# The second level of the RWKV join made for all four blocks of 32, with one evacuation each, and the norm's bias added with the bonus

## The chip, the cores and the metric

The kernel runs on one core of a Trainium2 chip. A core has a matrix engine, TensorE (PE in the profile; its weight loads are listed apart as PEld), three engines for elementwise work, VectorE (DVE), ScalarE (ACT) and GpSimd (POOL), and SyncE (SP), which issues most of the DMAs. Each engine takes its own instructions in the order of the program and stops where one of them has to wait. The metric is the device time of one execution in microseconds; the median of three runs of the kernel before is 3190.79 us (3189.75 to 3197.08).

## The reference

The reference is a model of two parts: two layers of a first network (528 tokens, width 1024), and one layer of a second network. Every layer of the first projects the tokens, runs attention (MLA) and a bidirectional RWKV mixer beside each other, joins them and runs a mixture of experts. The change lies in the RWKV mixer alone. Cut to that:

```python
def step(S, inp):
    r_t, w_t, k_t, v_t, kk_t, b_t = inp
    sa = jnp.einsum('bhvk,bhk->bhv', S, kk_t)
    S = S * w_t[:, :, None, :] - sa[..., None] * b_t[:, :, None, :] + v_t[..., None] * k_t[:, :, None, :]
    return S, jnp.einsum('bhvk,bhk->bhv', S, r_t)
...
bonus = jnp.sum(rh * kd * r_k, -1, keepdims=True) * vh
...
y = y_f + y_b
mu = jnp.mean(y, -1, keepdims=True)
var = jnp.mean(jnp.square(y - mu), -1, keepdims=True)
yn = ((y - mu) * lax.rsqrt(var + RWKV_GN_EPS)).reshape(B, L, RW) * gn_g + gn_b
out = (yn + (bonus_f + bonus_b).reshape(B, L, RW)) * g
```

There are eight heads of 64, and the scan runs once forward and once backward.

## The kernel before

The scan is done in nine chunks of 64 tokens. Inside a chunk the recurrence is a triangular system with a matrix of 64x64 per head; the kernel computes the inverse T of that matrix, and with it the chunk becomes a few products. A unit is one pair of heads p (0 to 3) in one direction d, so a layer has eight units, 0 to 7, unit i being p = i // 2, d = i % 2. Both layers run the same program, so there are 16 units.

The work of a unit passes through these generators:

- `rwkv_front` (L744) makes the decays and keys. It uses ACT, POOL and DVE. Its scan is L779, its longest steps are L798 on DVE and L800 on POOL, which write the tile rbk; in the backward direction POOL adds the two directions' keys (L813) and DVE makes the bonus's product (L815). L751 scales the keys on ACT for a new pair of heads, and L776 is POOL's first step of it.
- `rwkv_gen` (L820) makes the products KR (L834, DVE) and the chunk matrices Z (L846 on PE, L849 on DVE). After the backward direction `rwkv_bonus` (L867) replaces v by the bonus.
- `rwkv_inv` (L911) inverts the diagonal blocks of 16x16 on DVE (L924, L926), with DMAs before and after it.
- `rwkv_join` (L940) makes T from them in two levels. The first joins blocks of 16 to blocks of 32 (tile TB: four blocks of 32 on the 128 partitions, two heads by two halves, times eight chunks). Its products are Q (L959) and U (L967); L962 and L968 evacuate them on DVE. The second level joins blocks of 32 to 64: Q2 (L979) and U2 (L987) are made for one of the two halves of each head, so for two of the four partition quarters. ACT evacuates the quarter of the first head (L981, L988), DVE that of the second (L982, L989). The diagonal of T comes from TB by two ACT instructions (L970), each with a mask for one half.
- `rwkv_kx` (L992) and `rwkv_solve` (L1007) apply T: PE's products L1016 read the tile rtt, which is T.
- `rwkv_scan` (L1033) runs over the chunks: PE's L1069 and L1072, with DVE's L1070 between two chunks.
- `rwkv_post` (L1086) runs once for a pair of heads: mean, variance, the norm's scale (L1106, DVE), its bias (L1112, POOL), the bonus (L1114, POOL), and the gate's product (PE) that DVE multiplies in (L1118). It does so half by half of the 528 tokens. For p = 3, which runs after the last unit, one DVE instruction (L1109) does bias and bonus.

In `rwkv` (L1122) PE and DVE are set to the order in which the code is written. `spread` interleaves the generators' steps, up to each `yield`, by the weights given with them. In unit i the streams are the chain (solve and scan of unit i), the work behind it (gen of i+2, kx of i+2, front of i+3), inv and join of unit i+1, and in units 2, 4 and 6 the post step of the pair before. Join 0 comes ahead of unit 0. ACT, POOL and SP, and everything outside this part, get their order from a scheduler when the program is built.

Of the kernel before, what the change touches and what calls it, by code (L numbers as in the profile page):

```python
# [115 lines left out]
class K:  # L116
# [749 lines left out]

    def rwkv_bonus(self, S, G):  # L867
        nc = self.nc
        bs, v = G["bs"], S["v"][G["p"]]
        for c0, n in HALVES:  # L870
            ps = self.pa("bo", "r")
            nc.tensor.matmul(ps[:, :n], lhsT=self.blk1, rhs=bs[:, c0:c0 + n], start=True, stop=True)
            vv = v[:, PAD + c0:PAD + c0 + n]
            nc.vector.tensor_tensor(out=vv, in0=ps[:, :n], in1=vv, op=ALU.mult)
        yield

# [63 lines left out]
    def rwkv_join(self, S, G):  # L940
# [8 lines left out]
        def q4(g):  # L949
            return slice(32 * g, 32 * g + 32)  # L950
# [17 lines left out]
        nc.vector.tensor_tensor(out=TB, in0=TB, in1=ps[:, :8], op=ALU.add)  # L968
        for e in range(2):
            nc.scalar.activation(out=T[:, 1:9, 32 * e:32 * e + 32], in_=TB, func=AF.Copy, scale=self.par32[:, e:e + 1])  # L970
        yield
# [4 lines left out]
        for c in range(8):  # L976
            for h in range(2):
                g = 2 * h
                nc.tensor.matmul(ps[q4(g + 1), c], lhsT=Zx[h][q4(g), c + 1, 32:64], rhs=D[q4(g), c], start=True, stop=True)  # L979
        Q = self.t("rq", (128, 8, 32))  # L980
        nc.scalar.copy(Q[q4(1)], ps[q4(1), :8])  # L981
        nc.vector.tensor_copy(Q[q4(3)], ps[q4(3), :8])  # L982
        yield
        ps = self.pa("U2", "r").rearrange("p (c t) -> p c t", t=32)
        for c in range(8):
            for g in (0, 2):
                nc.tensor.matmul(ps[q4(g), c], lhsT=Q[q4(g + 1), c], rhs=TB[q4(g + 1), c], start=True, stop=True)  # L987
        nc.scalar.copy(T[q4(0), 1:9, 32:64], ps[q4(0), :8])  # L988
        nc.vector.tensor_copy(T[q4(2), 1:9, 32:64], ps[q4(2), :8])  # L989
        yield  # L990
# [95 lines left out]
    def rwkv_post(self, li, p, S, role):  # L1086
# [15 lines left out]
        for c0, n in HALVES:  # L1102
            q = slice(c0, c0 + n)
            ps = self.pa("hb", role)
            nc.tensor.matmul(ps[:, :n], lhsT=self.sel[:2, 0], rhs=rn[:2, q], start=True, stop=True)
            nc.vector.scalar_tensor_tensor(out=y[:, q], in0=y[:, q], scalar=self.col(f"gng{li}", p), in1=ps[:, :n], op0=ALU.mult,  # L1106
                                           op1=ALU.mult)
            if p == 3:
                nc.vector.scalar_tensor_tensor(out=y[:, q], in0=y[:, q], scalar=self.col(f"gnb{li}", p), in1=v[:, q], op0=ALU.add,  # L1109
                                               op1=ALU.add)  # L1110
            else:
                nc.gpsimd.tensor_scalar(out=y[:, q], in0=y[:, q], scalar1=self.col(f"gnb{li}", p), scalar2=0.0, op0=ALU.add,  # L1112
                                        op1=ALU.add)
                nc.gpsimd.tensor_tensor(out=y[:, q], in0=y[:, q], in1=v[:, q], op=ALU.add)  # L1114
            ps = self.pa("g", role)
            nc.tensor.matmul(ps[:, :n], lhsT=S["g2"][:, p * 128:(p + 1) * 128], rhs=S["gd"][:, PAD + c0:PAD + c0 + n], start=True,
                             stop=True)
            nc.vector.tensor_tensor(out=out[:, q], in0=y[:, q], in1=ps[:, :n], op=ALU.mult)  # L1118
            yield
        S["out"].append(out)  # L1120

    def rwkv(self, li, u, rn, nb, freed):  # L1122
# [17 lines left out]
        def gen(i):  # L1140
            if i <= last:
                yield from self.rwkv_gen(li, S, G[i])
                if units[i][1]:
                    yield from self.rwkv_bonus(S, G[i])

# [1727 lines left out]
```

## Time and profile before

| what | value |
|---|---|
| median of three runs | 3190.79 us |
| the profiled execution's own time | 3186.1 us |
| its span | 3184.2 us |
| PE, busy (share of the span) | 2716.5 us (85%) |
| DVE, busy | 1559.3 us (49%) |
| POOL, busy | 1231.7 us (39%) |
| ACT, busy | 1085.6 us (34%) |
| RWKV stage of layer 0 | about 320 to 663 us |
| RWKV stage of layer 1 | about 1395 to 1728 us |

How to read it: the shares are means over stages with different limits. In a view of the order of time each line is one instruction or several of one kind merged (x64 at its end): start and length in us, engine, line of the kernel, operation, the tile written and the tiles read, the shape, and in brackets how long the engine had been idle before it and which instruction ended that wait. A wait for several things is put down to the one that came last. For PE every product of fp32 operands shows as two records. In the view of stretches a line gives the length, then the busy time of PE, PEld, DVE, ACT and POOL with their counts, the granted PE clock as a share of full speed, the busy share of the DMA engines and the rate.

### The profile page before, as it was taken

To read this page: it belongs to the slowest core of one execution; us is meant where nothing else is said; L and a number is where in the kernel's file an instruction comes from. 1 tells how busy PE (TensorE), PEld (TensorE's weight loads), DVE (VectorE), ACT (ScalarE), POOL (GpSimd) and SP (SyncE) were. 2 spreads that over 40 slices of the span, in tenths; PEclk is the share of its full clock that TensorE was granted. 3 is DMA by queue.
4 is the path that set the end of the run, shared out by engine and by line. 5 is a ranking of instruction groups with operands and counts; after the bars stand their busy time and mean duration, and the time that the engine had idled before them with its cause. 6 is when DMAs were issued, how large, how long until landed. Compare 5 with 4: busy or idle time off the path is not lost. (4 is left out here: it accounts for less than half of the span.)

```text
span 3184.2 us, 54720 instructions
## 1 busy us (share of the span) xinstructions
PE 2716.5 (85%) x21572; PEld 2070.2 (65%) x21572; DVE 1559.3 (49%) x3328; ACT 1085.6 (34%) x2377; POOL 1231.7 (39%) x1276
## 2 busy tenths in 40 slices
PE   6998777888799499977778797779888999999998
PEld 5887655664354388856656533267676788778886
DVE  6575665543123427666653511144866667344412
ACT  4233433211232322244322111143335665244431
POOL 3124233052344322332323311047865544555554
PEclk8997776787899699978778799989999999999999
DMA  6220100348899615211114599932121124423343
GB/s 188 60 90 19 24 13 12 107 147 319 339 364 382 224 47 160 78 32 19 16 56 157 195 415 420 372 135 84 61 72 34 61 70 146 146 86 97 96 123 103
DMA packets 224043, 443.17 MB, mean 139 GB/s; under 512 B 96576, under 2 KB 105152, under 8 KB 197136
## 3 DMA queue, kind: packets, MB, share of 16 engines
q1 hardware_dynamic: 209648, 407.76, 36.8%
q0 software_dynamic: 9216, 25.44, 2.1%
q10 hardware_dynamic: 4912, 6.34, 0.5%
q8 instruction: 175, 2.87, 0.4%
q14 instruction: 92, 0.75, 0.1%
HBM read 400.91 MB, written 46.61 MB: 141 GB/s over the span
## 5 line engine op out<-in xcount | busy, mean ns | idle before, releaser
L230 POOL TENSOR_TENSOR wl<-wr,wh 128x512 fp32r<-128x512 f32 x328 | 435.5, 1329 | 535.3 <-ACT wh L229 505.1
L229 ACT CAST wh<-wr 128x512 fp32r<-128x512 f32 x352 | 217.5, 619 | 551.2 <-PE mm L336 208.2
L335 PE MATMUL mm<-hh,wh 128*128 128x264 f32 x608 | 186.1, 306 | 19.2 <-ACT hf L290 13.0
L335 PE MATMUL mm<-h,wh 128*128 128x512 f32 x480 | 187.6, 391 | 2.2 <-ACT h L229 2.2
L337 PE MATMUL mm<-h,wl 128*128 128x512 f32 x480 | 187.7, 391 | 1.2 <-POOL wl L230 1.2
L336 PE MATMUL mm<-h,wh 128*128 128x512 f32 x480 | 187.4, 390 | 0.3 <-DVE h L230 0.3
L337 PE MATMUL mm<-hh,wl 128*128 128x264 f32 x608 | 181.0, 298 | 0.0
L336 PE MATMUL mm<-hl,wh 128*128 128x264 f32 x608 | 179.5, 295 | 0.0
L1461 POOL DMA_INDIRECT ybuf<-my,rdst x32 | 32.3, 1009 | 278.5 <-DVE my L1460 247.6
L335 PEld LDWEIGHTS mm<-hh,wh 128*128 128x128 f32 x608 | 118.6, 195 | 29.6 <-ACT hf L290 13.6
L335 PE MATMUL go<-h,wh 128*128 128x512 f32 x288 | 121.1, 420 | 13.1 <-ACT th L2145 8.7
L1432 DVE SCALAR_TENSOR_TENSOR mth<-mth,w 128x256 f32<-128x256 f32 x32 | 13.5, 421 | 236.7 <-ACT mth L1431 236.7
L224 POOL TENSOR_SCALAR rs<-s 128x4 f32<-128x4 f32 (+7 forms) x62 | 14.7, 238 | 273.4 <-DVE s L723 196.0
L336 PEld LDWEIGHTS mm<-hl,wh 128*128 128x128 f32 x608 | 118.5, 195 | 2.6 <-issue 1.3
L337 PEld LDWEIGHTS mm<-hh,wl 128*128 128x128 f32 x608 | 118.3, 195 | 2.3 <-issue 1.3
L1443 PE MATMUL w<-mw,xT 128*64 128x512 f32 x344 | 113.7, 615 | 6.5 <-DMA mw<-in_moe_w_dram 6.3
L337 PE MATMUL go<-h,wl 128*128 128x512 f32 x288 | 116.1, 403 | 0.0
L336 PE MATMUL go<-h,wh 128*128 128x512 f32 x288 | 115.0, 399 | 0.0
L335 PEld LDWEIGHTS mm<-h,wh 128*128 128x128 f32 x480 | 90.5, 189 | 21.2 <-ACT h L229 2.5
L337 PEld LDWEIGHTS mm<-h,wl 128*128 128x128 f32 x480 | 90.4, 188 | 20.8 <-POOL wl L230 2.0
L336 PEld LDWEIGHTS mm<-h,wh 128*128 128x128 f32 x480 | 90.5, 189 | 19.4 <-issue 0.6
L1652 DVE SCALAR_TENSOR_TENSOR ma<-hf,sc,ma 128x512 f32<-128x512 f32 x112 | 94.5, 862 | 17.5 <-DMA hf<-in_w_mod_dram 16.8
(610 smaller groups left out, 7454.1 us busy)
## 6 DMA issues: line engine op xcount, KB each, us to landing
mw<-in_moe_w_dram SPq DMA_DIRECT2D x61, 1024.0 KB
mz<-in_moe_w_dram SPq DMA_DIRECT2D x48, 1024.0 KB
me<-in_moe_w_dram SPq DMA_DIRECT2D x47, 1024.0 KB
wr<-in_w_in_dram SPq DMA_DIRECT2D x176, 256.0 KB
mx<-in_moe_w_dram SPq DMA_DIRECT2D x36, 1024.0 KB
hf<-in_w_mod_dram SPq DMA_DIRECT2D x96, 256.0 KB
wr<-in_w_up_dram SPq DMA_DIRECT2D x88, 256.0 KB
wr<-in_w_down_dram SPq DMA_DIRECT2D x44, 256.0 KB
```

What stands on the lines that cost most here:

```text
L224: nc.gpsimd.tensor_scalar(out=a, in0=b, scalar1=float(mul), scalar2=float(eps), op0=ALU.mult, op1=ALU.add)
L229: self.nc.scalar.copy(hi, src)
L230: lo_eng.tensor_tensor(out=lo, in0=src, in1=hi.bitcast(F32), op=ALU.subtract)
L335: nc.tensor.matmul(out, lhsT=w[0], rhs=x[0], start=start, stop=False)
L336: nc.tensor.matmul(out, lhsT=w[0], rhs=x[1], start=False, stop=False)
L337: nc.tensor.matmul(out, lhsT=w[1], rhs=x[0], start=False, stop=stop)
L1432: nc.vector.scalar_tensor_tensor(out=th, in0=th, scalar=1.0, in1=p[:, 0:256], op0=ALU.add, op1=ALU.mult)
L1443: nc.tensor.matmul(p1[q], lhsT=xT[:, kt, q], rhs=w13[kt // 4][:, kt % 4], start=kt == 0, stop=kt == 7)
L1461: nc.gpsimd.indirect_dma_start(out=ybuf, out_offset=bass.IndirectOffsetOnAxis(ap=dst, axis=0), in_=y, in_offset=None, bounds_check=2 * L - ...
L1652: nc.vector.scalar_tensor_tensor(out=a, in0=w, scalar=sc[:, kt, c:c + 1], in1=a, op0=ALU.mult, op1=ALU.add)
```

## The change

Four things are done.

- In the join's second level Q2 and U2 are made for all four quarters. For the quarters that had no U2, the product of TB with an identity stands, so that U2 as a whole is the right half of T; for Q2 the two new quarters are computed and not used. One DVE instruction evacuates Q2, one ACT instruction evacuates U2 into T.
- One ACT instruction instead of two writes the diagonal from TB.
- The norm's bias is added to the bonus on POOL when the bonus is made (once for each pair of heads, over all 528 tokens), and no longer in the post step.
- The post step's last step is divided: first both halves get the norm's scale and the bonus, then, in a step of its own, both halves get the gate.

```diff
--- before.py
+++ after.py
@@ -864,7 +864,7 @@
             yield
         G.update(KR=KR, Zx=[z[:, :, 0] for z in ZB], BZ=[z[:, :, 1:3] for z in ZB], SV=SV)
 
-    def rwkv_bonus(self, S, G):
+    def rwkv_bonus(self, li, S, G):
         nc = self.nc
         bs, v = G["bs"], S["v"][G["p"]]
         for c0, n in HALVES:
@@ -872,6 +872,8 @@
             nc.tensor.matmul(ps[:, :n], lhsT=self.blk1, rhs=bs[:, c0:c0 + n], start=True, stop=True)
             vv = v[:, PAD + c0:PAD + c0 + n]
             nc.vector.tensor_tensor(out=vv, in0=ps[:, :n], in1=vv, op=ALU.mult)
+        vv = v[:, PAD:]
+        nc.gpsimd.tensor_scalar(out=vv, in0=vv, scalar1=self.col(f"gnb{li}", G["p"]), scalar2=0.0, op0=ALU.add, op1=ALU.add)
         yield
 
     def by_token(self, x, a, b, swap, scale=None):
@@ -966,27 +968,25 @@
             for g in range(4):
                 nc.tensor.matmul(ps[q4(g), c], lhsT=Q[q4(g), c], rhs=TB[q4(g), c], start=True, stop=True)
         nc.vector.tensor_tensor(out=TB, in0=TB, in1=ps[:, :8], op=ALU.add)
-        for e in range(2):
-            nc.scalar.activation(out=T[:, 1:9, 32 * e:32 * e + 32], in_=TB, func=AF.Copy, scale=self.par32[:, e:e + 1])
+        nc.scalar.activation(out=T[:, 1:9, 0:32], in_=TB, func=AF.Copy, scale=self.par32[:, 0:1])
         yield
 
         D = self.t("rq", (128, 8, 32))
         nc.vector.transpose(out=D, in_=TB)
         ps = self.pa("Q2", "r").rearrange("p (c t) -> p c t", t=32)
         for c in range(8):
-            for h in range(2):
-                g = 2 * h
-                nc.tensor.matmul(ps[q4(g + 1), c], lhsT=Zx[h][q4(g), c + 1, 32:64], rhs=D[q4(g), c], start=True, stop=True)
+            for g in range(4):
+                o = q4(g ^ 1)
+                nc.tensor.matmul(ps[o, c], lhsT=Zx[g // 2][q4(g), c + 1, 32:64], rhs=D[q4(g), c], start=True, stop=True)
         Q = self.t("rq", (128, 8, 32))
-        nc.scalar.copy(Q[q4(1)], ps[q4(1), :8])
-        nc.vector.tensor_copy(Q[q4(3)], ps[q4(3), :8])
+        nc.vector.tensor_copy(Q, ps[:, :8])
         yield
         ps = self.pa("U2", "r").rearrange("p (c t) -> p c t", t=32)
         for c in range(8):
-            for g in (0, 2):
-                nc.tensor.matmul(ps[q4(g), c], lhsT=Q[q4(g + 1), c], rhs=TB[q4(g + 1), c], start=True, stop=True)
-        nc.scalar.copy(T[q4(0), 1:9, 32:64], ps[q4(0), :8])
-        nc.vector.tensor_copy(T[q4(2), 1:9, 32:64], ps[q4(2), :8])
+            for g in range(4):
+                e = q4(g | 1)
+                nc.tensor.matmul(ps[q4(g), c], lhsT=self.ident[e, e] if g % 2 else Q[e, c], rhs=TB[e, c], start=True, stop=True)
+        nc.scalar.copy(T[:, 1:9, 32:64], ps[:, :8])
         yield
 
     def rwkv_kx(self, G):
@@ -1105,18 +1105,14 @@
             nc.tensor.matmul(ps[:, :n], lhsT=self.sel[:2, 0], rhs=rn[:2, q], start=True, stop=True)
             nc.vector.scalar_tensor_tensor(out=y[:, q], in0=y[:, q], scalar=self.col(f"gng{li}", p), in1=ps[:, :n], op0=ALU.mult,
                                            op1=ALU.mult)
-            if p == 3:
-                nc.vector.scalar_tensor_tensor(out=y[:, q], in0=y[:, q], scalar=self.col(f"gnb{li}", p), in1=v[:, q], op0=ALU.add,
-                                               op1=ALU.add)
-            else:
-                nc.gpsimd.tensor_scalar(out=y[:, q], in0=y[:, q], scalar1=self.col(f"gnb{li}", p), scalar2=0.0, op0=ALU.add,
-                                        op1=ALU.add)
-                nc.gpsimd.tensor_tensor(out=y[:, q], in0=y[:, q], in1=v[:, q], op=ALU.add)
+            (nc.vector if p == 3 else nc.gpsimd).tensor_tensor(out=y[:, q], in0=y[:, q], in1=v[:, q], op=ALU.add)
+        yield
+        for c0, n in HALVES:
+            q = slice(c0, c0 + n)
             ps = self.pa("g", role)
             nc.tensor.matmul(ps[:, :n], lhsT=S["g2"][:, p * 128:(p + 1) * 128], rhs=S["gd"][:, PAD + c0:PAD + c0 + n], start=True,
                              stop=True)
             nc.vector.tensor_tensor(out=out[:, q], in0=y[:, q], in1=ps[:, :n], op=ALU.mult)
-            yield
         S["out"].append(out)
 
     def rwkv(self, li, u, rn, nb, freed):
@@ -1141,7 +1137,7 @@
             if i <= last:
                 yield from self.rwkv_gen(li, S, G[i])
                 if units[i][1]:
-                    yield from self.rwkv_bonus(S, G[i])
+                    yield from self.rwkv_bonus(li, S, G[i])
 
         def kx(i):
             return self.rwkv_kx(G[i]) if i <= last else iter(())
```

In the changed kernel the first level's L954, L959, L962, L967 and L968 are L956, L961, L964, L969 and L970. The diagonal's L970 is L971, the transpose L974 is L975, Q2 is L980 with its copy L982, U2 is L988 with its copy L989. The bias is L876, the bonus's sum is L1108, the gate's product is L1115.

DVE, unit 2 of layer 0, at the first half of the post step of the first pair of heads (ryy is its scan result, ur takes the post step's output, rzb is the scan's state, rtb is TB). Before:

```order
L1070 TENSOR_SCALAR rzb_3154<-E_4466,s_3026 128x64 x2
L1106 SCALAR_TENSOR_TENSOR ryy_3745<-ryy_3745,pv,hb_4631 128x264
L1118 TENSOR_TENSOR ur_1684<-ryy_3745,g_4636 128x264
L968 TENSOR_TENSOR rtb_4443<-rtb_4443,U_4641 128x256
L1070 TENSOR_SCALAR rzb_3154<-E_4466,s_3026 128x64
```

Changed:

```order
L1070 TENSOR_SCALAR rzb_3155<-E_4555,s_3026 128x64 x2
L1106 SCALAR_TENSOR_TENSOR ryy_3789<-ryy_3789,pv,hb_4720 128x264
L1106 SCALAR_TENSOR_TENSOR ryy_3789<-ryy_3789,pv,hb_4724 128x264
L970 TENSOR_TENSOR rtb_4532<-rtb_4532,U_4730 128x256
L1070 TENSOR_SCALAR rzb_3155<-E_4555,s_3026 128x64
```

The gate's product has left this place, and the second half's scale stands there instead.

DVE, the same unit, from the transpose of the second level to the next unit's KR (rq are the transpose and Q2, rbk and rkd the front's results, rtt is T, rkr is KR). Before:

```order
L974 STREAM_TRANSPOSE rq_4702<-rtb_4443 128x256
L982 COPY rq_4721<-Q_886_4704 32x256
L798 SCALAR_TENSOR_TENSOR rbk_4724<-rt_4698,rt_4692 64x9x64 x2
L1070 TENSOR_SCALAR rzb_3154<-E_4466,s_3026 128x64
L1106 SCALAR_TENSOR_TENSOR ryy_3745<-ryy_3745,pv,hb_4737 128x264
L1118 TENSOR_TENSOR ur_1684<-ryy_3745,g_4742 128x264
L815 SCALAR_TENSOR_TENSOR rkd_4247<-ur_1820,pv,rkd_4247 128x528
L989 COPY rtt_2731<-U_893_4751 32x8x32
L920 MEMSET rnt_4770 72x16
L834 TENSOR_TENSOR rkr_4773<-rkk_4100,rt_4691 128x576
```

Changed:

```order
L975 STREAM_TRANSPOSE rq_4790<-rtb_4532 128x256
L982 COPY rq_4825<-Q_886_4792 128x256
L798 SCALAR_TENSOR_TENSOR rbk_4827<-rt_4786,rt_4780 64x9x64 x2
L1070 TENSOR_SCALAR rzb_3155<-E_4555,s_3026 128x64
L1115 TENSOR_TENSOR ur_1684<-ryy_3789,g_4840 128x264
L1115 TENSOR_TENSOR ur_1684<-ryy_3789,g_4843 128x264
L815 SCALAR_TENSOR_TENSOR rkd_4336<-ur_1820,pv,rkd_4336 128x528
L922 MEMSET rnt_4886 72x16
L834 TENSOR_TENSOR rkr_4889<-rkk_4160,rt_4779 128x576
```

The copy of Q2 has grown from 32 to 128 partitions, the gate's two products stand together after the scan's last chunk, and the copy into rtt is gone.

ACT, unit 0 of layer 0, around the join of unit 1 (rtt is T, rkk the keys that L751 scales, ryy the scan's result, rw and rsv what the solve makes). Before:

```order
L970 ACTIVATE rtt_2731<-rtb_3511,par_145 128x8x32 x2
L981 COPY rq_3734<-Q_725_3717 32x256
L1081 COPY ryy_3745<-Y_3557 128x512
L988 COPY rtt_2731<-U_728_3748 32x8x32
L885 COPY rsv_3774<-tok_3775 64x4x64 x2
L751 ACTIVATE rkk_5102<-u_2160,pv 128x576
L1017 COPY rw_2729<-WC_3782 128x192
```

Changed:

```order
L971 ACTIVATE rtt_2731<-rtb_3541,par_145 128x8x32
L1081 COPY ryy_3789<-Y_3587 128x512
L751 ACTIVATE rkk_5219<-u_2160,pv 128x576
L989 COPY rtt_2731<-U_728_3792 128x8x32
L887 COPY rsv_3833<-tok_3834 64x4x64 x2
L1017 COPY rw_2729<-WC_3841 128x192
```

The copy of U2 into T, which stood right behind the scan's result, now stands behind L751, and one of the two masked copies and the copy of Q2 are gone.

On POOL the bias add stands directly ahead of the L776 with which the front of the next unit begins (for the last pair of heads, ahead of the post step's L224).

## Rows read from the trace of the kernel before

**Rows 1.** The page: span and number of instructions.

```profile
span 3184.2 us, 54720 instructions
```

**Rows 2.** Busy times by stretch: length, five engines, granted clock, DMA share, GB/s.

```profile
320.00:663.00 343.00, 273.80 (x4203) 214.11 (x4203) 187.81 (x528) 116.29 (x306) 77.90 (x83) 0.75 0.16 42
1395.00:1728.00 333.00, 262.98 (x4203) 206.14 (x4203) 187.22 (x530) 116.10 (x306) 78.02 (x83) 0.77 0.17 44
2200.00:2350.00 150.00, 129.51 (x2211) 106.32 (x2210) 115.10 (x195) 46.95 (x154) 119.22 (x144) 0.93 0.18 60
```

**Rows 3.** Who waited for whom, whole span: us in total, times, longest.

```profile
DVE ur L1118 <- POOL ryy L1114: 32.8, 12, 3.9
...
DVE rq L982 <- ACT rq L981: 30.3, 16, 2.6
...
PE WC L1016 <- DVE rtt L989: 18.0, 8, 2.3
```

**Rows 4.** Order of time in unit 1: start, length, engine, line, operation, idle before.

```profile
406.28 1.06 PE L979 MATMUL Q<-rq,rzb 32*32 32x32 f32 x32 [0.62 <-DVE rq L974]
...
407.44 0.36 ACT L981 COPY rq<-Q 32x256 f32<-32x256 f32 x1 [1.87 <-PE Q L979]
...
407.83 0.43 DVE L982 COPY rq<-Q 32x256 f32<-32x256 f32 x1 [1.70 <-ACT rq L981]
...
411.88 0.36 ACT L988 COPY rtt<-U 32x256 f32<-32x256 f32 x1
...
412.36 2.88 DVE L798 SCALAR_TENSOR_TENSOR rbk<-rt,rt 64x576 f32<-64x576 f32 x2
...
415.27 0.42 DVE L989 COPY rtt<-U 32x256 f32<-32x256 f32 x1
...
415.75 1.11 PE L1016 MATMUL WC<-rkx,rtt 64*64 64x128 f32 x6 [2.17 <-DVE rtt L989]
...
422.64 1.02 DVE L849 TENSOR_TENSOR rzb<-Z,msk 128x384 f32<-128x384 f32 x2 [0.36 <-PE Z L846]
```

**Rows 5.** Order of time in unit 2, the same columns.

```profile
442.64 0.49 DVE L1106 SCALAR_TENSOR_TENSOR ryy<-ryy,pv,hb 128x264 f32<-128x264 f32 x1 [0.54 <-PE hb L1105]
...
445.27 0.43 DVE L1118 TENSOR_TENSOR ur<-ryy,g 128x264 f32<-128x264 f32 x1 [2.14 <-POOL ryy L1114]
...
445.95 0.28 DVE L1070 TENSOR_SCALAR rzb<-E,s 128x64 f32<-128x64 f32 x1
...
448.83 1.06 PE L979 MATMUL Q<-rq,rzb 32*32 32x32 f32 x32 [2.10 <-ACT rt L784]
...
451.29 0.43 DVE L982 COPY rq<-Q 32x256 f32<-32x256 f32 x1 [2.60 <-ACT rq L981]
...
456.62 1.30 POOL L813 TENSOR_TENSOR rkd<-rkd,rt 128x528 f32<-128x528 f32 x1
...
459.92 0.43 DVE L1118 TENSOR_TENSOR ur<-ryy,g 128x264 f32<-128x264 f32 x1 [3.93 <-POOL ryy L1114]
...
461.54 0.74 DVE L834 TENSOR_TENSOR rkr<-rkk,rt 128x576 f32<-128x576 f32 x1
```

**Rows 6.** Order of time: U, its evacuation, and scores in block 2.

```profile
401.30 1.07 PE L967 MATMUL U<-rtb,rq 32*32 32x32 f32 x64
...
402.44 0.42 DVE L968 TENSOR_TENSOR rtb<-rtb,U 128x256 f32<-128x256 f32 x1 [2.58 <-PE U L967]
...
2214.43 0.52 PE L2070 MATMUL sc<-gz 128*32 128x32 f32 x36
```

**Rows 7.** POOL: order of time before L776, and the instructions of L1112.

```profile
401.97 0.67 POOL L776 TENSOR_SCALAR rt<-rt 128x576 f32<-128x576 f32 x1 [26.07 <-ACT rt L770]
...
L1112 POOL TENSOR_SCALAR ryy<-ryy,pv x12: 1161/1168/1180, 443.2 to 1675.8; 128x264 f32<-128x264 f32 x12
```

**Rows 8.** Order of time in unit 0: the solve and L751.

```profile
377.15 1.55 PE L1016 MATMUL WC<-rkx,rtt 64*64 64x128 f32 x12
...
378.61 0.78 ACT L751 ACTIVATE rkk<-u,pv 128x576 f32<-128x576 f32 x1 [0.61 <-DVE rkr L834]
```

## The prediction

> **What bounds the kernel now.** I read the page first, then busy times by stretch, then who waited for whom, then the order of time inside single units of the two RWKV stages. The page gives a span of 3184.2 us [rows 1]; the profiled execution took 3186.1 us, 1.9 us around the span, and the median of the three runs shown lies 4.7 us above it. The sum below is made against 3186.1.
>
> The change touches the two RWKV stages (343 and 333 us [rows 2]) and nothing else in the source. There no engine is full: PE counts as busy 274 and 263 us at a mean granted clock of 0.75 and 0.77, DVE 188 and 187 us. What the reader is to see in these rows is that the stage is paced neither by one engine's sum nor by DMA (share 0.16 and 0.17), but by engines that run in a fixed order and stop for each other. So I price waits in the place where they stand. The waits that the edits touch [rows 3]: DVE waits 32.8 us for POOL before the last product of the post step (12 times), 30.3 us at its half of the copy of Q2, all 16 times behind ACT's half, and PE's solve waits 18.0 us for DVE's half of the copy into T. Part of each is a wait for work that must be done anyway, so these sums are no gain yet.
>
> A layer has eight units, 0 to 7. In unit i the chain solves and scans unit i, and beside it run the join of unit i+1, the front and generation of later units, and in units 2, 4 and 6 the post step of the pair before. Join 0 stands ahead of unit 0, so there are eight joins a layer, 16 in all.
>
> **Units 1 and 3 (no post step; four in two layers).** [Rows 4]: Q2's products end at 406.28 + 1.06 = 407.34; ACT copies a quarter at 407.44, and DVE starts its quarter at 407.83, after ACT. One DVE copy of all four quarters can start where ACT started: 0.39 us earlier. Then DVE has no gap of note until the 0.36 us before L849 at 422.64. In that run stands L989, 0.42 us and 0.06 until PE goes on, which leaves DVE: 0.46. T is complete at 412.24 (ACT's end) in place of 415.69, because DVE's half was queued behind L798; that lets PE start the solve 3.45 us earlier, but DVE's own queue is full, so of this I count only the 0.36 us gap. Sum 0.39 + 0.46 + 0.36 = 1.2 us a unit, 4.8 in four. Bounds: 0.39 if only the copy moves, 3.45 if the solve paced it.
>
> **Units 2 and 4 (with a post step; four in two layers).** [Rows 5]: DVE ends the first L1106 at 443.13 and stands idle 2.14 us until POOL has added bias and bonus; behind it wait the U evacuation and the scan's L1070. Now the second L1106 (0.49) comes there and no POOL result is wanted: 2.14 - 0.49 = 1.65 us earlier. Q2 ends at 449.89, DVE's copy started at 451.29 because ACT was busy with other work first; without ACT it can start at 450.0, 1.29 earlier. The second L1118 waited 3.93 us, since POOL took the post step's two operations only after L813. Now both L1118 find their input long done, and what is late next is L813: POOL's chain hangs on the scan step that went 1.65 us earlier, so L813 ends at 457.92 - 1.65 = 456.3. Between L1118 at 459.92 and L834 at 461.54 lie 1.62 us, of which L1118 (0.43) goes ahead and L989 (0.46) falls away; about 0.8 remains after L813. L834 then starts at 457.1 in place of 461.54: 4.4, taken as 4.3 us a unit, 17.2 in four. Bounds: 1.65, if the later waits come back elsewhere; 6.4, if POOL's chain does not hold (2.14 + 1.29 + 3.93, less the 0.49 and 0.43 of work that stays).
>
> **Units 5 and 6 and the join ahead of unit 0 (six).** No L798 stands between ACT's and DVE's half there; only the serial halves go: 0.39 + 0.46 = 0.85 each, 5.1. The third post step, in unit 6, gains about 0.5 more, twice: 1.0. Bounds 0.39, and 1.7 (1.29 + 0.46) if ACT was late there too, as in rows 5.
>
> **Unit 0 (two): a loss.** In ACT's order the copy into T now stands behind L751, which waits for DVE's L834 [rows 8]: before, T was complete by the time PE started its solve at 377.15. DVE reaches L834 sooner, by 0.5 (L989 gone) to 1.1 us (also its wait gone), so L751 ends at 378.61 + 0.78 - 1.1 = 378.3, the copy takes 0.36, the solve starts near 378.7: 1.5 us later, 3.0 in two. Bounds: a gain of 0.85, a loss of 2.2.
>
> **What is added.** A DVE copy of 128x256 in place of 32x256: the evacuation of 128x256 took 0.42 us against 0.43 [rows 6, 4], so nothing, and ACT's likewise. The rule to use both ScalarE and VectorE for PSUM evacuation (the Trainium skill, TensorEngine Tiling (Array Packing), PSUM Bottleneck) speaks against one copy. The rows disagree with it here: a quarter costs DVE what the whole costs, and the two quarters ran one after the other.
>
> 512 more products of 32x32. Per join PE issues 64 records in place of 32, over four squares of the array in place of two. Five microseconds apart, 64 records over four squares took 1.07 us and 32 over two took 1.06 [rows 6, 4]: no cost. In U2, however, two squares share their 32 rows. The nearest row is L2070, where four strips of columns share all 128 rows: 36 in 0.52 us, 14 ns each, against 17 ns each for the 64 squares that share nothing [rows 6]. So I take nothing; the other end, each pair strictly in turn, is the 1.06 us once more per join. It cannot be below nothing, since the products come on top.
> The Trainium skill (TensorE: Matmul & The Clock Gate, Part 3, What overlaps and what doesn't) says a weight load overlaps running products only if its row group differs; by that U2 pays up to 1.06 us. L2070's 14 ns disagree: its loads share all row groups.
>
> Eight bias adds on POOL (L876 of the changed kernel, 528 elements) in place of twelve of 264. Price between 0.6 us (L776, 0.67 for 576) and 2.3 (twice L1112's 1.17 [rows 7]); I take 2.3, the same two operations. They hide in POOL's idle time ahead of L776, 26.07 us in the unit shown; the order puts them directly before it. Uncovered they would cost 8 x 2.3 = 18.7. The last post step of a layer, on DVE, swaps one operation for one of the same size, and its four products share one PSUM buffer before and after: 0, within 1 us.
>
> No DMA of the stages is added or passed. Outside them a scheduler chose the order anew, most of all in 2200 to 2350, where PE is idle 150 - 129.5 = 20.5 us [rows 2]. The same work stands there with pieces exchanged: 0, within 5 us either way.
>
> **Sum.** 4.8 + 17.2 + 6.1 - 3.0 = 25.1 us: 3161.0 for an execution like the profiled one, up to 3166 at the level of the median; I say 3164. What follows a stage starts when it ends, so I carry the gain to the end whole. All lower bounds together give 4 x 0.39 + 4 x 1.65 + 6 x 0.39 - 4.4 = 6 us; all upper ones 4 x 3.45 + 4 x 6.4 + 6 x 1.7 + 1.7 = 51.
>
> **Rivals.**
> Waits refill. The other streams of a unit are as long as the chain, so a wait gone on DVE comes back at the next meeting point. For it: PE and DVE alternate without slack over most of a unit. Against: in rows 5 DVE's idle time is POOL's doing, and nothing else stands late there. The lower bounds hold, with unit 0's loss as taken: 4 x 0.39 + 4 x 1.65 + 6 x 0.39 - 3.0 = 7.5 us, so 3178.6, or 3183 at the median's level.
> U2 in turn. 1.06 us where T is wanted at once: unit 0, units 5 and 6, join 0, eight joins, 8.5 us; in units 1 to 4 the solve has over 2 us of slack. Gain 16.6: 3169.5 against the profiled execution, 3174 at the median's level. For it: the squares of a pair take the same rows. Against it L2070.
> More is gained, if in units 1 and 3 the solve was the pace: 25.1 + 4 x 2.25 = 34, so 3152.
> The clock (the slower case). Granted clock in the stages averages 0.76, which is a mixture of the two levels, 1.2 and 2.4 GHz; PE is busy 537 us in them. A fall of the mean to 0.70 would lengthen that by 537 x (0.76/0.70 - 1) = 46 us: 3186 - 25 + 46 = 3207. It decides below 0.714, where 35 us are lost. For it: mixtures of work so fine leave the clock to the order. Against it: the waits that go are partly PE's own, so PE becomes busier, not idler.
>
> **How the numbers follow.** Forecast 0.62, refilled waits 0.15, U2 in turn 0.08, more gained 0.08, clock 0.07. A measurement tells no less than 0.3% (9.6 us) from no change. Faster: 0.62 + 0.08 + 0.08 + 0.06 of the refilled case = 0.84; within 0.3%: the other 0.09 of it; slower 0.07. The range reaches from the case of more gained, 3150, to the refilled one at the median's level, 3183.
>
> **What would show it.** L1118 without a wait for POOL and the second one directly behind the first; in units 2 and 4 L834 about 4 us earlier after the first L1106; in units 1 and 3 PE's solve 3 us or more ahead of where DVE lets it use that; in unit 0 the solve later, behind L751; both stages 12 to 13 us shorter and the rest unchanged. U2's 64 records in 1.06 us or in 2.1. I am wrong if the stages shrink by under 5 us each, if the time comes or goes in 2200 to 2350, or if the granted clock of the stages moves.

## The result and the profile after

| | median | runs | profiled execution | span |
|---|---|---|---|---|
| before | 3193.26 us | 4 (3189.75 to 3197.08) | 3186.1 us | 3184.2 us |
| changed | 3159.47 us | 4 (3157.08 to 3160.03) | 3157.08 us | 3155.1 us |

The ratio is 0.9893, with a 95% interval of 0.9875 to 0.9910: the change gives 34 us (29 to 40). The forecast was 25 us and 3164 in a range of 3150 to 3183. So direction and time came true, and 9 us more came than the sum had.

The page of the changed kernel, and the stretches that answer to [rows 2] (columns as there):

```profile
span 3155.1 us, 56739 instructions
...
323.00:640.50 317.50, 261.36 (x4715) 205.95 (x4715) 182.13 (x520) 109.85 (x290) 80.90 (x81) 0.80 0.18 48
1383.00:1699.30 316.30, 258.67 (x4715) 205.10 (x4715) 182.89 (x522) 110.18 (x290) 81.28 (x81) 0.80 0.18 47
2174.50:2321.50 147.00, 125.31 (x2197) 105.27 (x2196) 116.09 (x195) 46.12 (x152) 117.67 (x143) 0.91 0.18 58
```

In this pair of executions the two stages are 25.5 and 16.7 us shorter and their mean granted clock is higher (0.80 against 0.75 and 0.77). The spans differ by only 29.1 us, because the program between the stages and ahead of them, whose source is unaltered, took 13 us longer. There the profiled execution of before was at its fast end: from the last product of unit 7's solve in layer 0 to the second transpose of join 0 in layer 1 it took 802.3 us, while the twelve other profiles of this document took 806.6 to 815.1. A repeat of the changed kernel (below) shows that such sums move by several microseconds with the clock from one execution to the next. So I read the gain from stretches inside a unit, between two instructions that depend on each other.

The waits that answer to [rows 3] (who waited for whom: us in total, times, longest):

```profile
DVE rq L982 <- PE Q L980: 19.6, 16, 1.5
...
DVE ur L1115 <- PE g L1113: 7.2, 10, 1.3
...
DVE rkd L815 <- POOL rkd L813: 26.2, 8, 5.1
...
PE WC L1016 <- ACT rtt L989: 1.4, 2, 1.1
```

DVE no longer waits for POOL at the gate (32.8 us before), nor for ACT at Q2's copy (30.3): at both places it now waits for PE, 7.2 and 19.6 us. The wait for POOL has for the most part moved: at L815 DVE waits 26.2 us for L813, where it waited 6.2 us before. The solve's 18.0 us behind DVE's copy have become 1.4 us behind ACT's.

Unit 2 of layer 0, the same columns as [rows 5]:

```profile
441.55 0.89 DVE L1106 SCALAR_TENSOR_TENSOR ryy<-ryy,pv,hb 128x264 f32<-128x264 f32 x2 [0.54 <-PE hb L1105]
...
445.54 0.43 DVE L975 STREAM_TRANSPOSE rq<-rtb 128x256 f32<-128x256 f32 x1
...
446.12 1.08 PE L980 MATMUL Q<-rq,rzb 32*32 32x32 f32 x64 [1.91 <-ACT rt L784]
...
447.25 0.42 DVE L982 COPY rq<-Q 128x256 f32<-128x256 f32 x1 [1.28 <-PE Q L980]
...
451.36 0.37 ACT L989 COPY rtt<-U 128x256 f32<-128x256 f32 x1 [0.44 <-PE U L988]
...
452.27 1.55 PE L1016 MATMUL WC<-rkx,rtt 64*64 64x128 f32 x12
...
454.17 1.31 POOL L813 TENSOR_TENSOR rkd<-rkd,rt 128x528 f32<-128x528 f32 x1
...
455.51 0.77 DVE L815 SCALAR_TENSOR_TENSOR rkd<-ur,pv,rkd 128x528 f32<-128x528 f32 x1 [5.10 <-POOL rkd L813]
...
456.22 0.74 DVE L834 TENSOR_TENSOR rkr<-rkk,rt 128x576 f32<-128x576 f32 x1
...
457.77 1.70 PE L846 MATMUL Z<-rkr,rbk 64*128 64x128 f32 x24 [0.96 <-DVE rpr L926]
...
460.16 1.01 DVE L849 TENSOR_TENSOR rzb<-Z,msk 128x384 f32<-128x384 f32 x2
```

L834 stands 456.22 - 441.55 = 14.67 us behind the first L1106; in [rows 5] it was 461.54 - 442.64 = 18.90. That is 4.23 less, where 4.4 was worked out and 4.3 taken. What is late next is L813, as foreseen. But the next mask, L849, gained more. These are two further rows of the kernel before, in the same unit (DVE):

```profile
448.24 0.44 DVE L974 STREAM_TRANSPOSE rq<-rtb 128x256 f32<-128x256 f32 x1
...
468.06 1.02 DVE L849 TENSOR_TENSOR rzb<-Z,msk 128x384 f32<-128x384 f32 x2 [2.51 <-PE Z L846]
```

From L834 to L849 it took 468.06 - 461.54 = 6.52 us before and 460.16 - 456.22 = 3.94 now. Before, PE was still at the solve when KR was ready, and the mask waited 2.51 us for the products Z. Now the solve starts at 452.27 while DVE waits for POOL, and Z can follow KR at once.

The same stretches in all units, by start times on DVE (the second transpose L974, now L975, to the next mask L849; for joins 0, 6 and 7 to the solve's last L1016). In each line the first unit comes first, in layer 0 and layer 1, then the second unit:

| stretch | change in us | sum | forecast |
|---|---|---|---|
| units 2, 4: first L1106 to transpose | -1.61, -1.61, -1.57, -1.61 | -6.4 | -6.6 |
| units 2, 4: transpose to L834 | -2.62, -2.63, -2.89, -2.90 | -11.0 | -10.6 |
| units 2, 4: L834 to mask | -2.58, -2.06, -1.24, -1.20 | -7.1 | 0 |
| units 1, 3: transpose to mask | -1.47, -1.63, -2.28, -2.10 | -7.5 | -4.8 |
| unit 0: transpose to mask | +2.36, +1.73 | +4.1 | +3.0 |
| join 0; joins 6, 7 | +0.59, -0.67; -2.62 to +0.24 | -4.2 | -6.1 |
| all | | -32.1 | -25.1 |

The sum of the stretches, 32.1 us, agrees with the 34 (29 to 40) of the medians, and the line that the forecast lacked is the third. Before, the mask waited 2.51, 1.98, 1.16 and 1.12 us for Z in these four units; now it does not wait for Z in any of them, and the third line is as long as these waits.

The stretches leave out the rest of each unit. From the second transpose of join 0 to the solve's last product of unit 7 the two layers took 41.8 us less in this pair of profiles and 35.6 less in the repeat, so 9.7 and 4.6 us went outside the stretches. In the other profiles below this remainder lies between -5 and +10 us. What it consists of is not shown.

### The profile page after: what moved, and what is told of

Its sections match the earlier page's. It is cut to its first block, busy times and chain, and to the rows that moved or that the text cites. A ratio compares the mean times of both kernels' runs of the same rounds, so it can differ in the third digit from the quotient of the medians.

```text
span 3155.1 us, 56739 instructions
## 1 busy us (share of the span) xinstructions
PE 2705.5 (86%) x22596; PEld 2062.0 (65%) x22596; DVE 1558.1 (49%) x3312; ACT 1073.4 (34%) x2345; POOL 1241.0 (39%) x1272
## 5 line engine op out<-in xcount | busy, mean ns | idle before, releaser
L224 POOL TENSOR_SCALAR rs<-s 128x4 f32<-128x4 f32 (+7 forms) x62 | 14.5, 236 | 237.2 <-DVE s L723 159.6
```

## Experiments

Each ratio is to the kernel before on the same chip, with its 95% interval; "stretches" is the sum of the table's last line for that kernel.

**The two parts apart.** First the join alone: bias, bonus and post step as before (the main edits, against the changed kernel).

```diff
-        vv = v[:, PAD:]
-        nc.gpsimd.tensor_scalar(out=vv, in0=vv, scalar1=self.col(f"gnb{li}", G["p"]), ...)
...
+                nc.gpsimd.tensor_scalar(out=y[:, q], in0=y[:, q], scalar1=self.col(f"gnb{li}", p), ...)
+                nc.gpsimd.tensor_tensor(out=y[:, q], in0=y[:, q], in1=v[:, q], op=ALU.add)
```

> The join's second level as in the changed kernel, bias and post step as before. In the changed kernel the two stages became 43 us shorter and 14 us came back outside them. By the waits (W, the prediction's steps): units 1 and 3 4.8, units 5 and 6 and join 0 5.1, unit 0 -3.0, and in units 2 and 4 only the copy that leaves DVE, 4 x 0.46 = 1.8, since the second gate product still waits for POOL: 8.7 us, ratio 0.997. By the clock (C): whatever takes waits away lifts the granted clock of the stages from 0.75 to 0.78 and brings some 17 us on top: 26 us of stage, ratio 0.992 to 0.995. By the join (D): the surplus over the forecast is the join's: over 20 us of stage at an unchanged clock.

Measured: 0.9956 (0.9942 to 0.9971), 14 us; stretches -16.3. In units 2 and 4, L834 moves by 0.32, 0.33, 0.58 and 0.57 us, as W has it (0.46), since the second gate product, here L1116, now waits 7.65 us for POOL, where it waited 3.93 [rows 5]:

```profile
453.72 0.42 DVE L980 COPY rq<-Q 128x256 f32<-128x256 f32 x1 [1.28 <-PE Q L978]
...
463.93 0.43 DVE L1116 TENSOR_TENSOR ur<-ryy,g 128x264 f32<-128x264 f32 x1 [7.65 <-POOL ryy L1112]
...
464.98 0.74 DVE L834 TENSOR_TENSOR rkr<-rkk,rt 128x576 f32<-128x576 f32 x1
```

But L834 to mask is 3.94 us here too, so those 7.1 us are the join's. D is right on where the surplus is and wrong on its size.

Then the post step and the bias alone, with the join of before (the main edits, against the changed kernel).

```diff
-        nc.vector.tensor_copy(Q, ps[:, :8])
+        nc.scalar.copy(Q[q4(1)], ps[q4(1), :8])
+        nc.vector.tensor_copy(Q[q4(3)], ps[q4(3), :8])
...
-        nc.scalar.copy(T[:, 1:9, 32:64], ps[:, :8])
+        nc.scalar.copy(T[q4(0), 1:9, 32:64], ps[q4(0), :8])
+        nc.vector.tensor_copy(T[q4(2), 1:9, 32:64], ps[q4(2), :8])
```

> Bias with the bonus and the post step's last step divided as in the changed kernel, the join as before. W: units 2 and 4 give 4.3 less the 0.46 of the copy that stays on DVE, 4 x 3.84 = 15.4, and the third post step 1.0: 16.4 us, ratio 0.995; units 0, 1 and 3 unchanged. C: a clock of 0.78 in the stages and 17 us more: 33 us of stage. D (the surplus is the join's): no more than 16 us of stage. With the join alone the two add up to the change's 43 us of stage if the parts are independent; to less if what one gives the other gives too.

Measured: 0.9929 (0.9906 to 0.9953), 23 us; stretches -16.7. First L1106 to L834 falls by 3.82 to 3.93 us in the four units (W 3.84), L834 to mask by 0.0 in sum. The two parts together give 16.3 + 16.7 = 33.0 us by the stretches and 37 by the ratios, the change 32.1 and 34: they add up, and no 17 us of clock come on top of each. The granted clock from 320 to 640 and from 1395 to 1700 us was 0.77 and 0.76 with the join alone, 0.74 and 0.78 with the post step alone, beside 0.75 and 0.77 in the stages of before, so it was not lifted as C has it. C falls.

Next the post step's part divided again, both with the join of before (edits against the kernel before). Only the division:

```diff
                 nc.gpsimd.tensor_tensor(out=y[:, q], in0=y[:, q], in1=v[:, q], op=ALU.add)
+        yield
+        for c0, n in HALVES:
+            q = slice(c0, c0 + n)
             ps = self.pa("g", role)
...
-            yield
```

> Only the post step's last step is divided; the bias stays in the post step on POOL, half by half, and the join is as before. W: DVE no longer waits 2.14 us at the first gate product and 3.93 at the second, but POOL now does both halves' bias and bonus (3.8 us in place of 1.9) ahead of its L780, about 1.1 us late for the scan, and L813 is late by as much: 3.84 - 1.1 = 2.7 us in each of four units, 11 us with the third post step 12, ratio 0.996. Rival: POOL hides its four operations, then as much as with the bias moved, 16 us, 0.995.

Measured: 0.9963 (0.9949 to 0.9977), 12 us. First L1106 to L834 falls by 2.53 to 2.60 us (W 2.7); the rival's 3.84 does not come. L834 to mask grows by 2.3 us in sum, so the stretches give 7.2. Only the bias:

```diff
+        nc.gpsimd.tensor_scalar(out=vv, in0=vv, scalar1=self.col(f"gnb{li}", G["p"]), ...)
...
-                nc.gpsimd.tensor_scalar(out=y[:, q], in0=y[:, q], scalar1=self.col(f"gnb{li}", p), ...)
```

> Only the bias is added with the bonus; the post step keeps both halves' gate products in turn, and the join is as before. W: the first gate product waits 0.97 in place of 2.14 us (1.17 less, and L813 comes earlier by as much), the second is still behind L813 on POOL but with one operation less, 1.17: 2.3 us in each of four units, 9.4 us, ratio 0.997. Rival: the second wait comes only from L813, so that only 1.17 a unit goes: 4.7 us, 0.9985. Second rival: the eight adds on POOL are not hidden and cost up to 16 us: ratio over 1.000.

Measured: 0.9970 (0.9954 to 0.9987), 10 us; first L1106 to L834 falls by 2.53 to 2.56 us (W 2.3); L834 to mask grows by 2.3 us here too; stretches -7.3. Neither rival comes: by these rows 10.2 us went in the four units, where the first rival had 4.7, and the adds did not cost 16.

**Does a stretch repeat?** The changed kernel, unaltered.

> The changed kernel once more, unaltered, to see which stretches of a unit repeat and which move with the clock. By the waits (W): from the second transpose of a join to the next mask on DVE each unit repeats within 0.5 us (units 2 and 4: 14.6 and 13.6 us), while the whole stages, whose granted clock is another each time, move by up to 10 us; ratio to before 0.989. By the clock (C): the stretches move as the stages do.

Measured: 0.9891 (0.9866 to 0.9916). The second stage with its lead-in, in the first execution and in this one:

```profile
1348.30:1699.20 350.90, 281.19 (x4859) 222.34 (x4856) 206.30 (x560) 124.75 (x325) 101.52 (x101) 0.79 0.17 43
```

```profile
1348.40:1705.70 357.30, 286.95 (x4859) 225.24 (x4856) 205.47 (x560) 124.74 (x324) 101.44 (x100) 0.77 0.17 43
```

The same program takes 6.4 us more at a lower granted clock, PE 5.8 us more of busy time. The stretch to the mask in units 2 and 4 is the same within 0.02 us, in units 0, 1 and 3 within 0.4 (W); for joins 0, 6 and 7, it moves by up to 2. So the 42.2 us of stage in the one pair of profiles were no better a measure than the 29 of the spans.

**Is it the solve?** U2's copy into T on DVE, one instruction as before.

```diff
-        nc.scalar.copy(T[:, 1:9, 32:64], ps[:, :8])
+        nc.vector.tensor_copy(T[:, 1:9, 32:64], ps[:, :8])
```

> The changed kernel with U2's copy into T on DVE in place of ACT, still one instruction. On DVE it stands just ahead of KR, in units 2 and 4 behind the key product that waits for POOL, so T is complete some 4.5 and 2.5 us later there. If the surplus over the forecast comes from the solve being done by the time KR is ready (S): transpose to mask grows by 2.4 in unit 2 and 1.7 in unit 4, by 0.4 in units 1 and 3, and falls by 2 in unit 0, where the copy no longer waits for L751: +6 us in all, ratio 0.991. If the surplus has nothing to do with the solve (C): 0.4 in units 1 to 4, -2 in unit 0: -1 us, ratio 0.989.

Measured: 0.9903 (0.9885 to 0.9921), 31 us, which by itself does not tell S from C. The stretches do: transpose to mask is 17.59 and 16.31 us in unit 2 (14.62 in the changed kernel), 15.11 and 15.92 in unit 4 (13.57), and 11.55 and 10.16 in unit 0 (12.5). Unit 2 of layer 0:

```profile
458.98 0.69 PE L1016 MATMUL WC<-rkx,rtt 64*64 64x128 f32 x4
463.36 1.11 PE L1016 MATMUL WC<-rkx,rtt 64*64 64x128 f32 x8 [3.69 <-DVE rtt L989]
...
468.20 2.27 PE L846 MATMUL Z<-rkr,rbk 64*128 64x128 f32 x24
```

```profile
462.20 0.77 DVE L815 SCALAR_TENSOR_TENSOR rkd<-ur,pv,rkd 128x528 f32<-128x528 f32 x1 [5.08 <-POOL rkd L813]
462.88 0.42 DVE L989 COPY rtt<-U 128x256 f32<-128x256 f32 x1
463.24 0.74 DVE L834 TENSOR_TENSOR rkr<-rkk,rt 128x576 f32<-128x576 f32 x1
...
469.84 1.02 DVE L849 TENSOR_TENSOR rzb<-Z,msk 128x384 f32<-128x384 f32 x2 [2.59 <-PE Z L846]
```

With the copy behind L815 the solve stops for 3.69 us, KR is ready before the solve is, and the mask waits 2.59 us for Z, as the 2.51 of before. Units 1 and 3, for which S had 0.4 us more, are the same within 0.03 except one that grows by 0.33; the stretches sum to -25.5, so 6.6 us are lost where S had 6. S holds: the third line of the table comes from T being complete while DVE waits for POOL.

**The terms taken as nothing.** Without the bias add (the norm's bias is left out):

```diff
-        nc.gpsimd.tensor_scalar(out=vv, in0=vv, scalar1=self.col(f"gnb{li}", G["p"]), ...)
```

> The changed kernel without the bias add L876 (the norm's bias is left out of the computation). If POOL hides the eight adds of 2.06 us, as the prediction took: transpose to mask as in the changed kernel, ratio 0.989. Rival, the adds delay the front of the next unit: up to 8 x 2.06 = 16.5 us less, ratio 0.984.

Measured: 0.9891 (0.9868 to 0.9913); stretches -30.7, against -32.1 and -31.0 in the two profiles with it. The adds are hidden. The products alone, on the kernel before:

```diff
+            for g in range(4):
+                o = q4(g ^ 1)
+                nc.tensor.matmul(ps[o, c], lhsT=Zx[g // 2][q4(g), c + 1, 32:64], rhs=D[q4(g), c], ...)
...
+            for g in range(4):
+                e = q4(g | 1)
+                nc.tensor.matmul(ps[q4(g), c], lhsT=self.ident[e, e] if g % 2 else Q[e, c], rhs=TB[e, c], ...)
```

> The kernel before, with Q2's and U2's products made for all four quarters (512 more of 32x32), but only the quarters of before copied, by the two engines as before; the rest is not used. If they cost nothing (the prediction): Q2 and U2 in 64 records of 1.06 to 1.08 us, transpose to mask in units 1 to 4 as before within 0.3 us, ratio 1.000. Rival, in turn: 1.06 us a join, 8 to 17 us, ratio 1.003 to 1.005. A third: pauses of 0.3 to 1.3 us inside the 64 records, as three to five joins of the changed kernel show them: up to 3 us, 1.001.

Measured: 1.0018 (1.0002 to 1.0034), 6 us slower, with an interval from 1 to 11. Q2 and U2 take 1.07 to 1.14 us for 64 records where the clock is low, except for one U2 of 1.78 with a pause of 0.64; the stretches sum to -0.6. So the squares don't run in turn, and a small cost is there all the same; where it stands these traces don't show.

**Can the loss in unit 0 be had back?** U2's copy on DVE in unit 0 alone:

```diff
-        nc.scalar.copy(T[:, 1:9, 32:64], ps[:, :8])
+        (nc.vector.tensor_copy if first else nc.scalar.copy)(T[:, 1:9, 32:64], ps[:, :8])
...
+            return self.rwkv_join(S, G[i], i == 1) if i <= last else iter(())
```

> The changed kernel with U2's copy into T on DVE in unit 0 alone, elsewhere on ACT. W: unit 0 no longer loses to L751: transpose to mask falls from 12.5 towards the 10.1 to 10.8 of before, 1.7 to 2.4 us in each layer, 4 us in all, ratio 0.988. Rival: KR, one copy later on DVE, or the 64 products set the end in unit 0 and nothing comes back: 12.5, ratio 0.989.

Measured: 0.9875 (0.9855 to 0.9894). Unit 0's stretch is 11.53 and 10.20 us, 1.0 and 2.3 less. By the medians the gain over the changed kernel (0.9891 in the same session) isn't told from none.

Then the 5.10 us that DVE waits at L815 in the rows of unit 2 above. Its result is wanted only by the bonus, so it can stand behind the masks:

```diff
-            nc.vector.scalar_tensor_tensor(out=bs, in0=r[:, PAD:], scalar=self.col(f"rk{li}", p), in1=bs, ...)
...
             yield
+        if d:
+            bs = G["bs"]
+            nc.vector.scalar_tensor_tensor(out=bs, in0=r[:, PAD:], scalar=self.col(f"rk{li}", p), in1=bs, ...)
         for h in range(2):
```

> As the run with unit 0's copy on DVE, and the key product L815, for which DVE waits 5.1 us for POOL's L813 in unit 2, moved behind the masks of the same unit, so that KR and the inverse need not wait for POOL. W: KR comes 5 us earlier in units 2 and 4, but the solve then sets the mask: transpose to mask falls by 1.4 in unit 2 and 0.3 in unit 4, in sum 3.4 us, and up to 10 more if the inverse, which also starts earlier, was late for the next join: ratio 0.984 to 0.987. Rival: POOL's L800 or the inverse's DMAs are late next, and nothing is gained over the run without the move: 0.988.

Measured: 0.9840 (0.9821 to 0.9858), 3148.23 us beside 3163.02 for the changed kernel in the same session: the lowest median of all. Unit 2 of layer 0 (KR, Z and the masks stand two lines earlier in this kernel, the inverse and the solve two lines later; first DVE, then PE):

```profile
452.70 1.34 DVE L832 TENSOR_TENSOR rkr<-rkk,rt 128x576 f32<-128x576 f32 x1
453.96 1.95 DVE L832 TENSOR_TENSOR rkr<-ur,rt 128x576 f32<-128x576 f32 x1
455.84 1.37 DVE L928 TENSOR_TENSOR rpr<-rnt 72x14 f32<-72x14 f32 x1
...
457.45 1.18 DVE L928 TENSOR_TENSOR rpr<-rnt 72x26 f32<-72x26 f32 x1
...
460.66 1.01 DVE L847 TENSOR_TENSOR rzb<-Z,msk 128x384 f32<-128x384 f32 x2
```

```profile
457.78 1.33 PE L1018 MATMUL WC<-rkx,rtt 64*64 64x128 f32 x18
459.04 1.75 PE L844 MATMUL Z<-rkr,rbk 64*128 64x128 f32 x24
```

Transpose to mask falls by 1.8 us in unit 2 and by 1.0 and 0.4 in unit 4 (W 1.4 and 0.3), 5 us in all. Z now follows the solve without a gap. In unit 4 the mask waits 0.30 and 0.91 us for Z, so there the solve sets it, as W has it. In unit 2 it does not: DVE has no gap from KR to the mask, because two steps of the inverse (L928) take 1.37 and 1.18 us where they took 0.16 and 0.18 before, and the mask stands 12.82 us behind the transpose in both layers although Z starts at 11.21 in one and 10.65 in the other. The medians of this kernel and the last are 11 us apart; the rest is not placed.

The same move without unit 0's copy on DVE:

```diff
-        (nc.vector.tensor_copy if first else nc.scalar.copy)(T[:, 1:9, 32:64], ps[:, :8])
+        nc.scalar.copy(T[:, 1:9, 32:64], ps[:, :8])
```

> The changed kernel with the key product L815 moved behind the masks, and U2's copy on ACT in all units. W: in unit 0 DVE reaches KR 2.5 us earlier, L751 on ACT ends as much earlier, and the copy behind it no longer delays the solve: transpose to solve's last product falls from 11.2 to below 10, without the copy on DVE; ratio 0.984 as in the run with both. Rival: the copy on ACT still comes late and unit 0 keeps its loss of 4 us in two layers: 0.9855.

Measured: 0.9866 (0.9841 to 0.9891). In unit 0 the solve no longer stops for the copy, but its last product stands 10.62 and 10.35 us behind the transpose, not below 10, and the mask still comes 1.75 and 1.5 us later than before. W is half right, and the two kernels with the move aren't told apart.

## Why the prediction was right, and where it was short

- **First gate product** (1.65 us a unit): 1.57 to 1.61. Right.
- **Q2's copy without ACT, the second gate product, L989 off DVE** (the rest of 4.3 a unit, 2.65): 2.62 to 2.90, with L813 late next and 0.74 us from its end (POOL's L813 ends at 455.48) to L834, where 0.8 was taken. Right, and the two edits apart gave their parts.
- **What follows L834** (taken as nothing): 7.1 us in four units. This is the step that failed: "L834 then starts at 457.1 in place of 461.54: 4.4, taken as 4.3 us a unit" ends the count at L834. The text had seen that the solve runs ahead, but booked a gain from it only in a rival, and only for units 1 and 3; [rows 5] end at L834, and the 2.51 us for which the mask waited on Z stood one row further.
- **Units 1 and 3** (1.2 a unit): 1.47 to 2.28, more than the sum and less than the rival's 3.45. The solve is 3.4 us ahead as foreseen (its last product 12.40 us behind the transpose in unit 1, 15.77 before), and DVE's own queue sets the mask, with no gap before it: 8.44 us from L834 to L849 in all four, 6.79 to 7.61 before. The queue grew because KR and the inverse now come while POOL still works at L800. In unit 1 of layer 0 two steps of the inverse took 0.16 and 0.18 us before; now (DVE, then POOL, whose two products of L800 stand in one row):

```profile
417.59 1.37 DVE L926 TENSOR_TENSOR rpr<-rnt 72x14 f32<-72x14 f32 x1
...
419.20 1.28 DVE L926 TENSOR_TENSOR rpr<-rnt 72x26 f32<-72x26 f32 x1
...
423.07 1.01 DVE L849 TENSOR_TENSOR rzb<-Z,msk 128x384 f32<-128x384 f32 x2
```

```profile
417.13 3.31 POOL L800 TENSOR_TENSOR rbk<-rt,rt 64x576 f32<-64x576 f32 x2
```

  All four units show the two long steps, 2.3 us together; the gains stay 1.2 to 2.0 us under the rival's 3.45. No run takes the overlap away, so its share is not shown. The last section says what the overlap does.
- **Unit 0** (a loss of 1.5, twice): 2.36 and 1.73. Right in mechanism, though the copy is not the whole of it. With the copy on DVE 1.0 us of the loss comes back in layer 0 and all of it in layer 1. The solve's granted clock differs as well: 0.72 and 0.59 before, 0.51 and 0.50 in the changed kernel, 0.54 and 0.62 with the copy on DVE. And in layer 0 U2 takes 1.85 us with a pause (last section), 1.08 in layer 1. These rows of layer 0 show the mechanism beside [rows 8]; the copy ends behind L751, and the solve's second part waits for it:

```profile
378.32 0.78 ACT L751 ACTIVATE rkk<-u,pv 128x576 f32<-128x576 f32 x1 [2.05 <-DVE rkr L834]
...
379.00 0.35 ACT L989 COPY rtt<-U 128x256 f32<-128x256 f32 x1
...
379.41 1.12 PE L1016 MATMUL WC<-rkx,rtt 64*64 64x128 f32 x8 [0.32 <-ACT rtt L989]
```

- **Join 0, units 5 and 6, third post step** (6.1): 4.2, within what these stretches move by; a part of the third post step lies ahead of them and is not in the 4.2.
- **One copy for two** (nothing): right. The columns are the shortest, the middle and the longest time in ns; first DVE's, then ACT's copy. Against 429 and 361 for a quarter (0.43 and 0.36 in [rows 4]), the whole takes 4 ns less on DVE and 11 more on ACT:

```profile
L982 DVE COPY rq<-Q x16: 423/425/426, 347.3 to 1645.4; 128x256 f32<-128x256 f32 x16
```

```profile
L989 ACT COPY rtt<-U x16: 353/372/373, 349.0 to 1650.4; 128x256 f32<-128x256 f32 x16
```

- **Bias on POOL** (hidden; 2.3 us each): right, at 2.06 us:

```profile
L876 POOL TENSOR_SCALAR u<-u,pv x8: 2057/2060/2077, 333.4 to 1606.5; 128x528 f32<-128x528 f32 x8
```

- **512 products** (nothing): nearly; 6 us (1 to 11), and no turn-taking. If the changed kernel pays the 6 us too, the rest of the change is worth that much more. The argument from L2070, however, did not show it, so that the term came out near nothing was in part luck: L2070's 14 ns stand at a granted clock of 1.00 (2214.3 to 2215.0), the 17 ns of the squares that share nothing at 0.50 (401.2 to 402.4). At 1.00 such squares take 0.74 us for 64 (Q2 at 1408.15 in the changed kernel), 12 ns each, less than L2070's. What decides is U2 beside Q2 at one clock. The rule that a weight load overlaps running products only if its row group differs (the Trainium skill, TensorE: Matmul & The Clock Gate, Part 3, What overlaps and what doesn't) does not show in U2, whose pairs share their rows and take 1.07 us at a granted clock of 0.50, as Q2 does (1.08), whose squares share nothing.
- **The clock** ("I am wrong if the granted clock of the stages moves"): it moved, to 0.80, and the reasons held all the same. With 0.77 in place of 0.79 over the second stage and its lead-in, the second profile of the same kernel had the same stretches to the mask in units 2 and 4. It was no sound test, since it moves between executions of one program.

## What to carry to other kernels

Follow a removed wait to the next point where two engines meet, and not only to the first instruction that moves: the engine that had been waited for may finish early enough to free a second one. Before summing a whole stage from one profile of each kernel, look at the granted clock; here the stretches to the masks of units 0 to 4 repeated within 0.4 us, and the sum of a stage did not. Look for an instruction that waits in a queue while its result is wanted much later: moving L815 shortened the stretches of units 2 and 4 by a further 5 us.

## What the runs showed of the hardware that was not expected

Some of DVE's instructions take longer while POOL works beside them. In the changed kernel's unit 2, where POOL was idle, KR's two took 0.74 and 0.75 us; in the run with the key product later, 1.34 and 1.95, beside these on POOL (L800 is two, of 1.80 and 1.81):

```profile
452.01 1.41 POOL L793 TENSOR_TENSOR rt<-rt,u 128x576 f32<-128x576 f32 x1
453.50 3.68 POOL L800 TENSOR_TENSOR rbk<-rt,rt 64x576 f32<-64x576 f32 x2
```

L793 ends at 453.42 and KR's first at 454.04; the first L800 ends at 455.30 and KR's second at 455.91. Each DVE instruction ends 0.61 to 0.62 us behind POOL's, so most of its 0.74 ran only then. The same holds for all 24 products of KR in this profile that took over 0.8 us: each ends 0.60 to 0.62 us behind an instruction of POOL. That is a turn for a whole instruction, as the Trainium skill has it for the port pair that VectorE and GpSimd share (SBUF — State Buffer, SBUF: two separate sides): whoever starts first holds it to its end. It is not so beside every instruction of POOL: in the changed kernel L876, which reads SBUF too, ran from 333.40 to 335.48 by its record, and KR's two beside it, from 334.26, took 0.74 and 0.75. Why L876 differs was not tested. For the forecast the turns mean that a DVE instruction which moves in time can shrink or grow by a microsecond, which the sum had nowhere.

The 64 records of U2 pause in some joins, 0.2 to 1.3 us. In unit 0 of layer 0 the pause comes after the 50th record in the changed kernel (both profiles), with the join alone, without the bias add and in the two with a copy into T on DVE; with the key product moved it comes after the 49th. The changed kernel:

```profile
376.23 0.29 PE L988 MATMUL U<-rtb,rq 32*32 32x32 f32 x2
376.99 0.26 PE L988 MATMUL U<-rtb,ident 32*32 32x32 f32 x1 [0.47 <-issue]
```

With the products on the kernel before, the pause stands elsewhere. So it seems to belong to a place in the program and not to the products; what it is was not tested.
